# Sample state update of a gated recurrence by pairs of heads on four row groups of TensorE, in a one-core decoder layer

## The chip, the cores and the metric

The kernel runs on one core of a Trainium2 chip. Its time is device microseconds of one execution; the figure used is the median of several runs. Each execution of the program is one launch.

## What is computed

The reference is one layer of a hybrid decoder for a prompt group (1 x 1024 tokens) and a sample group (8 sequences x 8 tokens) that share weights: a first SwiGLU block, a mixer, a second SwiGLU block. The mixer projects with `w_in`, runs sliding-window attention on one part and a gated linear recurrence with four heads on another, and projects back with `w_out`. Everything is f32. The part that matters here is the recurrence (`hgrn2_chunked`) of the sample group, whose state (8 sequences x 4 heads x 128 x 128) comes in as `state_hgrn` and goes out updated:

```
A = jnp.einsum('bhtk,bhsk,bhtsk->bhts', qb, kb, decay)
o = jnp.einsum('bhts,bhsv->bhtv', A, vb) + jnp.einsum('bhtk,bhkv->bhtv', qb * jnp.exp(G), S)
S = jnp.exp(G_last[:, :, 0, :])[..., None] * S + jnp.einsum('bhsk,bhsv->bhkv', kb * jnp.exp(G_last - G), vb)
```

For a sample sequence there is one chunk of 8 tokens: the new state of a head is its old state, scaled row by row, plus keys (8 x 128) transposed times values (8 x 128).

## The kernel before, in words

**Tiling.** Tokens are cut into three blocks: block 0 holds 256 prompt tokens and the 64 sample tokens (width 320), blocks 1 and 2 hold 384 prompt tokens each. Projections are done as three products of split f32 halves (`mm3`, L276 to L280): one full-array matmul each on L278, L279 and L280. These carry most of the time of TensorE.

**Order.** The source is written as one stream of projection and FFN units with generators beside it. `stream` and `tick` (L96 to L107) let a generator (the mixer of a block, normalisations) advance by one step at fixed rates while units go by. A scheduler of the framework then orders the instructions of each engine by its own model of time and gives tiles their slots; an instruction whose slot is not free is put later. So what stands together in the source need not stand together on the engine. Each engine then runs its list in order and waits on semaphores. SP issues nearly all transfers, in order.

**Banks.** PSUM has eight banks of 128 x 512 f32: four with the tag `mm` (`mmbank`, L60) for the projections, four with the tag `ax` (`axbank`, L63) for everything that the generators do. Around the change the projections in turn are those of block 1: `w_in_units(1)` (L1049). Its `tr` (L1054) is a unit of 24 matmuls of 384 columns into one `mm` bank, taken out by VectorE on L1060; the value projection (L1098 to L1108) uses three `mm` banks at once for 72 matmuls of 512 columns. Weights come by SP in 512 KB loads into three raw slots and are split by ScalarE (L257) and VectorE (L258).

**The sample update.** `sample_hgrn` (L1401) runs as part of the mixer of block 0, beside `sample_attn` (L1322), whose output goes through DRAM (`osc`, L1390 and L1395) before `finish_attn` (L1121) ends it, and beside the normalisation of block 1 (`pre_n`, L443, its transposes on L467). `intra` (L1207) makes the chunk's inner products `At`, the scaled queries `Q`, keys `K` and the decay `D`, all with channels on the 128 partitions. Then:
- L1409 transposes the keys of the four heads, each 128 x 64 to 64 x 128, into one bank; L1411 copies them to `kn` (64 partitions, tokens).
- For each head `a`: L1415 loads its state (512 KB); L1417 (GpSimd) masks the queries by sequence; L1420 (VectorE) builds `vb`, the head's values repeated four times and masked so that each copy keeps one sequence of each half (`seqm`, L200); L1425 and L1429 add the output products into `sav`, on halves of 32 tokens; L1431 (GpSimd) scales the state by `D`; L1435 multiplies keys and masked values of each half (32 rows, 512 columns: four sequences at once) into an `ax` bank, `su`; L1437 (VectorE) adds that to the state; L1438 stores it.

So the eight `su` products of L1435 use rows 0 to 31 and 32 to 63 of the array, the partitions on which the 64 sample tokens lie. The values come from the projection of block 0: `z["v"]`, third row tile, partitions 0 to 63 (L1106 to L1108).

Of the kernel before, what the change touches and what calls it, by code (L numbers as in the profile page):

```python
# [8 lines left out]
F32 = mybir.dt.float32  # L9
# [9 lines left out]
P = 128  # L19
# [25 lines left out]
def tile_step(ctx: ExitStack, tc: tile.TileContext, A: dict, O: list):  # L45
# [82 lines left out]
    amask = cp.tile([P, 256], F32, name="amask")  # L128
    smask = cp.tile([P, 136], F32, name="smask")
    ssink = cp.tile([P, 2], F32, name="ssink")  # L130
    seqm = cp.tile([NS, 4], F32, name="seqm")
    lmask = {h: cp.tile([P, 32], U8, name=f"lm{h}") for h in LEVELS[2:]}
    ident32 = cp.tile([P, 32], F32, name="ident32")
    lb = cp.tile([P, 4], F32, name="lb")
# [32 lines left out]
    def mix_consts():  # L167
# [852 lines left out]
    def mixing(tp, h):  # L1020
# [28 lines left out]
        def w_in_units(n):  # L1049
            w = WIDTH[n]  # L1050
            npb = NPB[n]
            z = Z[n] = {}

            def tr(c, dst):  # L1054
                wt = col_tile(c)
                bank = mmbank()
                proj(bank[:, :w], wt, h[n], w, range(4))
                tick()
                proj(bank[:, :w], wt, h[n], w, range(4, 8))
                V.tensor_scalar(dst, bank[:, :w], bias(c), None, op0=ALU.add)  # L1060
# [36 lines left out]
            S.activation(z["hq"][:, :, :w], z["hq"][:, :, :w], AF.Silu)  # L1097
            hv = z["v"] = big(F32, (P, 3, 512))  # L1098
            banks = [mmbank() for _ in range(nb)]
            for kk in range(4):  # L1100
                ap = w_in[kk * 256:(kk + 1) * 256, 1792:2304].rearrange("(k p) m -> p k m", p=P)
                wt = load_w([(None, ap)], pp, "wsp", 8, (P, 2, 512))
                proj_tok(banks, wt, h[n], n, (2 * kk, 2 * kk + 1))
                tick()
                tick()
            for i in range(nb):  # L1106
                r = rows_of(n, i)
                V.tensor_tensor(hv[:r, i], banks[i][:r], bhi[:r], op=ALU.add)  # L1108
# [98 lines left out]
        def intra(n, c0, r, top, last_q, res):  # L1207
# [193 lines left out]
        def sample_hgrn():  # L1401
# [2 lines left out]
            res = []  # L1404
            yield from intra(n, c0, r, 4, True, res)
            At, Q, K, D = res
            tb = axbank("skT").rearrange("p (a t) -> p a t", a=4)
            for a in range(4):
                PE.transpose(tb[:r, a], K[:, a, :r], ident)  # L1409
            kn = t2((P, 4, P))  # L1410
            V.tensor_copy(kn[:r], tb[:r])  # L1411
            ob = axbank("sav")
            for a in range(4):
                st = big(F32, (P, 8, P))
                nc.sync.dma_start(st, A["state_hgrn"][0][:, a].rearrange("b k v -> k b v"))  # L1415
                qm = t2((P, 2, 4, 32))
                G.tensor_tensor(qm, Q[:, a, :r].rearrange("p (f t) -> p f t", f=2).unsqueeze(2).to_broadcast(  # L1417
                    [P, 2, 4, 32]), own.unsqueeze(1).to_broadcast([P, 2, 4, 32]), op=ALU.mult)
                vb = t2((P, 4, P))
                V.tensor_tensor(vb[:r], z["v"][:r, 2, a * P:(a + 1) * P].unsqueeze(1).to_broadcast([r, 4, P]),  # L1420
                                seqm.unsqueeze(2).to_broadcast([r, 4, P]), op=ALU.mult)
                yield
                sr = [slice(32 * hf, 32 * hf + 32) for hf in range(2)]
                for hf in range(2):
                    PE.matmul(ob[sr[hf], a * P:(a + 1) * P], At[:r, a, sr[hf]], z["v"][:r, 2, a * P:(a + 1) * P],  # L1425
                              start=True, stop=False, skip_group_check=True)
                for b in range(4):
                    for hf in range(2):
                        PE.matmul(ob[sr[hf], a * P:(a + 1) * P], qm[:, hf, b], st[:, 4 * hf + b], start=False,  # L1429
                                  stop=b == 3, skip_group_check=True)  # L1430
                G.tensor_tensor(st, st, D[:, a].unsqueeze(2).to_broadcast([P, 8, P]), op=ALU.mult)  # L1431
                yield
                for hf in range(2):
                    ub = axbank("su").rearrange("p (b t) -> p b t", b=4)
                    PE.matmul(ub, kn[sr[hf], a], vb[sr[hf]], start=True, stop=True)  # L1435
# [283 lines left out]
```

## Time and profile before

| what | value |
|---|---|
| median of three runs | 2006.6 us (2004.51 to 2008.71) |
| the profiled execution | 2007.94 us |
| its span in the profile | 2006.2 us |
| granted TensorE clock over the span | 0.999 |
| mean DMA rate | 185 GB/s |

The profile is of one execution, and its span leaves out what lies around the program's own instructions. The page gives busy time of each engine, the chain of waits that ended last, and groups of instructions by source line; further views of the trace list instructions in order of time, tabulate windows, or follow the chain through a stretch. PE is TensorE's matmuls, PEld its weight loads, DVE VectorE, ACT ScalarE, POOL GpSimd, SP the engine that issues transfers. An f32 matmul with f32 operands shows as two records. Ends of matmuls are modelled and they overlap, so prices on TensorE are read from start to start.

### The profile page before, as it was taken

How to read it: one execution, taken by the hardware profiler on the slowest of the kernel's cores; microseconds unless marked ns; L12 is line 12 of the kernel's file. 1: busy time of each engine (PE TensorE's matmuls, PEld its weight loads, DVE VectorE, ACT ScalarE, POOL GpSimd, SP SyncE). 2: the span in 40 equal slices, each digit the busy share in tenths (PEclk: the TensorE clock that was granted, in tenths of full speed). 3: DMA queues.
4: the chain of work that ended last, by engine and by line, in shares of the span. 5: the costliest groups of instructions: out<-in, count | busy, mean ns of one | idle time of the engine just before them, and what ended most of it. 6: DMA issues, size and time to landing. Idle time of an engine off the chain costs nothing.

```text
span 2006.2 us, 34709 instructions
## 1 busy us (share of the span) xinstructions
PE 1983.4 (99%) x13349; PEld 1856.0 (93%) x13349; DVE 1410.5 (70%) x2303; ACT 934.5 (47%) x1689; POOL 541.5 (27%) x508
## 2 busy tenths in 40 slices
PE   9999999999999999999999999999999999999998
PEld 8999999999998987798899898988999999999886
DVE  6676667887558655777667756857888878655666
ACT  7544333444455434435344544746544444444452
POOL 0013443655104101211212311220155565510201
PEclk9999999999999999999999999999999999999999
DMA  8545446566766756766434243527566555577874
GB/s 259 169 122 179 132 129 215 202 221 226 235 217 219 190 150 215 256 166 190 135 93 144 85 143 106 175 89 235 153 198 211 184 192 192 208 231 234 285 260 138
DMA packets 377319, 370.31 MB, mean 185 GB/s; under 512 B 40546, under 2 KB 294321, under 8 KB 377137
## 3 DMA queue, kind: packets, MB, share of 16 engines
q1 hardware_dynamic: 371169, 357.21, 56.2%
q10 hardware_dynamic: 5984, 10.88, 1.6%
q8 instruction: 105, 1.72, 0.4%
q14 instruction: 61, 0.50, 0.1%
HBM read 284.31 MB, written 84.71 MB: 184 GB/s over the span
## 4 chain that ended last, share of the span: by engine, by line
PE 87%; DVE 5%; DMA 5%; ACT 2%; issue 2%; SPq 0%; DVEq 0%; ACTq 0%
PE mm L278 26%; PE mm L280 25%; PE mm L279 25%; DMA raw<-in_ffn_w_gu_dram 2%; DMA ar<-act 2%; PE pv L1196 1%; PE c L278 1%; PE c L280 1%; PE c L279 1%; PE sc L1155 1%; DVE t L707 1%; DVE w L258 1%; PE pT L1183 1%; DVE wspl L258 1%; DMA ar<-fa 1%
## 5 line engine op out<-in xcount | busy, mean ns | idle before, releaser
L278 PE MATMUL mm<-h,wsph 128*128 128x320 f32 (+1 forms) x1296 | 412.1, 320 | 2.9 <-ACT wsph L257 1.3
L280 PE MATMUL mm<-h,wspl 128*128 128x320 f32 (+1 forms) x1296 | 409.1, 317 | 1.9 <-DVE wspl L258 1.8
L279 PE MATMUL mm<-h,wsph 128*128 128x320 f32 (+1 forms) x1296 | 409.6, 317 | 0.4 <-DVE h L258 0.4
L257 ACT CAST wsph<-raw 128x1024 fp32r<-128x1024 f32 x202 | 211.4, 1049 | 280.5 <-PE mm L279 211.9
L258 DVE TENSOR_TENSOR wspl<-raw,wsph 128x1024 fp32r<-128x1024 f32 x202 | 253.1, 1257 | 123.3 <-ACT wsph L257 120.7
L258 DVE TENSOR_TENSOR w<-raw,w 128x512 fp32r<-128x512 f32 (+1 forms) x214 | 223.9, 1050 | 87.4 <-ACT w L257 86.0
L257 ACT CAST w<-raw 128x512 fp32r<-128x512 f32 (+1 forms) x214 | 158.1, 742 | 216.1 <-PE mm L279 111.7
L278 PEld LDWEIGHTS mm<-h,wsph 128*128 128x128 f32 x1296 | 242.8, 188 | 7.4 <-issue 2.5
L280 PEld LDWEIGHTS mm<-h,wspl 128*128 128x128 f32 x1296 | 243.0, 188 | 5.8 <-DVE wspl L258 2.7
L279 PEld LDWEIGHTS mm<-h,wsph 128*128 128x128 f32 x1296 | 243.3, 188 | 2.4 <-issue 1.1
L278 PE MATMUL mm<-h,w 128*128 128x384 f32 x704 | 235.4, 335 | 1.5 <-DVE big L761 1.5
L279 PE MATMUL mm<-h,w 128*128 128x384 f32 x704 | 235.6, 335 | 0.0
L280 PE MATMUL mm<-h,w 128*128 128x384 f32 x704 | 230.2, 335 | 0.0
L278 PE MATMUL mm<-w,h 128*128 128x512 f32 x462 | 181.0, 395 | 1.1 <-DVE big L956 1.1
L745 POOL TENSOR_TENSOR big<-big 128x384 f32<-128x384 f32 x88 | 113.4, 1288 | 252.5 <-ACT big L758 143.8
L279 PE MATMUL mm<-w,h 128*128 128x512 f32 x462 | 181.1, 392 | 0.0
L280 PE MATMUL mm<-w,h 128*128 128x512 f32 x462 | 179.7, 391 | 0.0
L278 PE MATMUL mm<-big,w 128*128 128x384 f32 x528 | 176.8, 335 | 1.9 <-ACT big L748 1.1
L279 PE MATMUL mm<-big,w 128*128 128x384 f32 x528 | 176.5, 334 | 0.0
L280 PE MATMUL mm<-big,w 128*128 128x384 f32 x528 | 176.4, 334 | 0.0
L258 DVE TENSOR_TENSOR w<-t,w 128x512 fp32r<-128x512 f32 x176 | 160.7, 922 | 10.7 <-ACT w L257 10.3
L278 PEld LDWEIGHTS mm<-h,w 128*128 128x128 f32 x704 | 132.1, 188 | 1.8 <-DVE big L761 1.8
(358 smaller groups left out, 3854.6 us busy)
## 6 DMA issues: line engine op xcount, KB each, us to landing
raw<-in_ffn_w_gu_dram SPq DMA_DIRECT2D x156, 512.0 KB
raw<-in_ffn_w_down_dram SPq DMA_DIRECT2D x74, 512.0 KB
raw<-in_w_in_dram SPq DMA_DIRECT2D x54, 512.0 KB
ar<-fa SPq DMA_DIRECT2D x70, 384.0 KB
big<-in_ffn_w_down_dram SPq DMA_DIRECT2D x88, 256.0 KB
fb<-big SPq DMA_DIRECT2D x44, 512.0 KB
fa<-big SPq DMA_DIRECT2D x22, 768.0 KB
raw<-fb SPq DMA_DIRECT2D x30, 512.0 KB
```

What stands on the lines that cost most here:

```text
L257: S.copy(hi, src)
L258: (lo_eng or V).tensor_tensor(lo, src, hi.bitcast(F32), op=ALU.subtract)
L278: PE.matmul(out, a[0], b[0], start=first, stop=False, skip_group_check=resume)
L279: PE.matmul(out, a[0], b[1], start=False, stop=False, skip_group_check=resume)
L280: PE.matmul(out, a[1], b[0], start=False, stop=last, skip_group_check=resume)
L707: V.tensor_tensor(t, x, y, op=ALU.subtract)
L745: G.tensor_tensor(e[:, i], e[:, i], e[:, i + 1], op=ALU.mult)
L1155: PE.matmul(banks[g][:, i * 256:i * 256 + wk], zq[64 * g:64 * g + 64, 2 * pr + i, b * P:(b + 1) * P], kx[64 * g:64 * g + 64, k0:k0 + wk], ...
L1183: PE.transpose(bank[:, (i * nk + kb) * P:(i * nk + kb + 1) * P], pt[g][:, i, kb * P:(kb + 1) * P], ident)
L1196: PE.matmul(ob[:, hd * 64:hd * 64 + 64], pT[g][:, (i * nk + kb) * P:(i * nk + kb + 1) * P], vn[:, vb, g * 64:g * 64 + 64], start=kb == 0, ...
```

## The change

The four heads are taken in two pairs. The even head's keys and values stay on partitions 0 to 63; the odd head's go to partitions 64 to 127.
- After the value projection of block 0, one transfer on SP copies the values of heads 1 and 3 (64 x 2 x 128, 64 KB) from partitions 0 to 63 to the unused partitions 64 to 127 of the same tile, at the place of heads 0 and 2.
- `seqm` is built for 128 partitions instead of 64.
- `K` is made 64 wide for the sample block, so that the keys of two heads lie next to each other. Two transposes of 128 x 128 take the place of four of 128 x 64, and the copy to `kn` is 128 x 256 instead of 64 x 512.
- `vb` is built once for a pair, on 128 partitions, ahead of both heads' steps: two builds instead of four.
- Within a pair, both heads' output products and state scalings come first. The four `su` products follow, on rows 0, 32, 64 and 96 of the array, into two `ax` banks and two `mm` banks. Then come the four additions, with a store of each head's state after its second one. The even head's products go to the `ax` banks, the odd head's to the `mm` banks.

```diff
-    seqm = cp.tile([NS, 4], F32, name="seqm")
+    seqm = cp.tile([P, 4], F32, name="seqm")
...
-        V.tensor_scalar(seqm, tf[:NS, 3, 0:4], tf[:NS, 2, 64:65], None, op0=ALU.is_equal)
+        V.tensor_scalar(seqm, tf[:, 3, 0:4], tf[:, 2, 64:65], None, op0=ALU.is_equal)
...
                 V.tensor_tensor(hv[:r, i], banks[i][:r], bhi[:r], op=ALU.add)
+            if n == 0:
+
+                odd, even = [hv[sl, 2].rearrange("p (q o c) -> p q o c", o=2, c=P) for sl in (slice(0, NS), slice(NS, P))]
+                nc.sync.dma_start(even[:, :, 0], odd[:, :, 1])
...
-            Q, K, D = t2((P, 4, P)), t2((P, 4, P)), t2()
+            Q, K, D = t2((P, 4, P)), t2((P, 4, r)), t2()
...
-            for a in range(4):
-                PE.transpose(tb[:r, a], K[:, a, :r], ident)
-            kn = t2((P, 4, P))
-            V.tensor_copy(kn[:r], tb[:r])
+            for p in range(2):
+                PE.transpose(tb[:, p], K[:, 2 * p:2 * p + 2].rearrange("p a t -> p (a t)"), ident)
+            kn = t2((P, 2, P))
+            V.tensor_copy(kn, tb[:, :2])
...
-                vb = t2((P, 4, P))
-                V.tensor_tensor(vb[:r], z["v"][:r, 2, a * P:(a + 1) * P].unsqueeze(1).to_broadcast([r, 4, P]),
-                                seqm.unsqueeze(2).to_broadcast([r, 4, P]), op=ALU.mult)
...
+            for p in range(2):
+                vb, sts = t2((P, 4, P)), []
+                V.tensor_tensor(vb, z["v"][:, 2, 2 * p * P:2 * p * P + P].unsqueeze(1).to_broadcast([P, 4, P]),
+                                seqm.unsqueeze(2).to_broadcast([P, 4, P]), op=ALU.mult)
+                for a in (2 * p, 2 * p + 1):
...
-                for hf in range(2):
-                    ub = axbank("su").rearrange("p (b t) -> p b t", b=4)
-                    PE.matmul(ub, kn[sr[hf], a], vb[sr[hf]], start=True, stop=True)
-                    sl = st[:, 4 * hf:4 * hf + 4]
-                    V.tensor_tensor(sl, sl, ub, op=ALU.add)
-                nc.sync.dma_start(O[7][0][:, a].rearrange("b k v -> k b v"), st)
+                ubs = [axbank("su"), axbank("su"), mmbank(), mmbank()]
+                for i, ub in enumerate(ubs):
+                    rows = slice(32 * i, 32 * i + 32)
+                    PE.matmul(ub, kn[rows, p], vb[rows], start=True, stop=True)
+                for i, ub in enumerate(ubs):
+                    sl = sts[i // 2][:, 4 * (i % 2):4 * (i % 2) + 4]
+                    V.tensor_tensor(sl, sl, ub.rearrange("p (b t) -> p b t", b=4), op=ALU.add)
+                    if i % 2:
+                        nc.sync.dma_start(O[7][0][:, 2 * p + i // 2].rearrange("b k v -> k b v"), sts[i // 2])
```

The output products, the query masks and the scalings of the state keep their form inside the head's steps.

More of the change, by code (lines that the diff above doesn't have):

```diff
@@ L1407, in sample_hgrn @@
             tb = axbank("skT").rearrange("p (a t) -> p a t", a=4)
-            for a in range(4):
-                PE.transpose(tb[:r, a], K[:, a, :r], ident)
-            kn = t2((P, 4, P))
-            V.tensor_copy(kn[:r], tb[:r])
+            for p in range(2):
+                PE.transpose(tb[:, p], K[:, 2 * p:2 * p + 2].rearrange("p a t -> p (a t)"), ident)
+            kn = t2((P, 2, P))
+            V.tensor_copy(kn, tb[:, :2])
             ob = axbank("sav")
[L1413 to L1418, printed above, removed]
-                vb = t2((P, 4, P))
-                V.tensor_tensor(vb[:r], z["v"][:r, 2, a * P:(a + 1) * P].unsqueeze(1).to_broadcast([r, 4, P]),
-                                seqm.unsqueeze(2).to_broadcast([r, 4, P]), op=ALU.mult)
-                yield
-                sr = [slice(32 * hf, 32 * hf + 32) for hf in range(2)]
-                for hf in range(2):
-                    PE.matmul(ob[sr[hf], a * P:(a + 1) * P], At[:r, a, sr[hf]], z["v"][:r, 2, a * P:(a + 1) * P],
-                              start=True, stop=False, skip_group_check=True)
-                for b in range(4):
-                    for hf in range(2):
[L1429 to L1433, printed above, removed]
-                    ub = axbank("su").rearrange("p (b t) -> p b t", b=4)
-                    PE.matmul(ub, kn[sr[hf], a], vb[sr[hf]], start=True, stop=True)
-                    sl = st[:, 4 * hf:4 * hf + 4]
-                    V.tensor_tensor(sl, sl, ub, op=ALU.add)
-                nc.sync.dma_start(O[7][0][:, a].rearrange("b k v -> k b v"), st)
@@ new lines, in sample_hgrn @@
+            sr = [slice(32 * hf, 32 * hf + 32) for hf in range(2)]
+            for p in range(2):
[3 more added lines that the diff above has]
+                for a in (2 * p, 2 * p + 1):
+                    st = big(F32, (P, 8, P))
+                    sts.append(st)
+                    nc.sync.dma_start(st, A["state_hgrn"][0][:, a].rearrange("b k v -> k b v"))
+                    qm = t2((P, 2, 4, 32))
+                    G.tensor_tensor(qm, Q[:, a, :r].rearrange("p (f t) -> p f t", f=2).unsqueeze(2).to_broadcast(
+                        [P, 2, 4, 32]), own.unsqueeze(1).to_broadcast([P, 2, 4, 32]), op=ALU.mult)
+                    yield
+                    for hf in range(2):
+                        PE.matmul(ob[sr[hf], a * P:(a + 1) * P], At[:r, a, sr[hf]], z["v"][:r, 2, a * P:(a + 1) * P],
+                                  start=True, stop=False, skip_group_check=True)
+                    for b in range(4):
+                        for hf in range(2):
+                            PE.matmul(ob[sr[hf], a * P:(a + 1) * P], qm[:, hf, b], st[:, 4 * hf + b], start=False,
+                                      stop=b == 3, skip_group_check=True)
+                    G.tensor_tensor(st, st, D[:, a].unsqueeze(2).to_broadcast([P, 8, P]), op=ALU.mult)
+                    yield
+                ubs = [axbank("su"), axbank("su"), mmbank(), mmbank()]
[7 more added lines that the diff above has]
+                        nc.sync.dma_start(O[7][0][:, 2 * p + i // 2].rearrange("b k v -> k b v"), sts[i // 2])
```

## The prediction

> **What bounds the kernel now.** I read the page first: the busy shares and the chain that ended last.
>
> ```profile
> span 2006.2 us, 34709 instructions
> PE 1983.4 (99%) x13349; PEld 1856.0 (93%) x13349; DVE 1410.5 (70%) x2303; ACT 934.5 (47%) x1689; POOL 541.5 (27%) x508
> PE 87%; DVE 5%; DMA 5%; ACT 2%; issue 2%; SPq 0%; DVEq 0%; ACTq 0%
> ```
>
> TensorE is busy for all but 23 us, and 87% of the chain is its own work. That is an average, so I asked for the stretch that the change touches: from the keys' transposes (L1409, at 902.40) to the last instruction that the update feeds (L1282, over by 981.45), as a table of windows.
>
> ```profile
> 902.40:981.45 79.05, 79.05 (x500) 65.80 (x498) 57.12 (x115) 37.20 (x64) 14.39 (x17) 1.00 0.60 176
> 912.70:933.00 20.30, 20.30 (x162) 16.57 (x160) 19.23 (x45) 12.52 (x19) 3.94 (x3) 1.00 0.76 220
> ```
>
> The columns are length, then busy time of PE, PEld, DVE, ACT and POOL, granted clock, DMA share, GB/s. TensorE has no idle moment in 79 us and runs at full clock. VectorE is close behind between 912.7 and 933 (19.23 of 20.30 us), but TensorE does not wait for it. So a step here is worth what it adds to or takes from TensorE's queue, as long as no new wait appears. Then I asked for the chain of waits over 890 to 1000; it stays on TensorE in this stretch, and names each piece of the sample update:
>
> ```profile
> 913.96 1.00 PE sav L1429 x16
> ...
> 920.53 1.06 PE su L1435 x4
> ...
> 929.57 0.78 PE sav L1429 x12
> ...
> 931.38 0.34 PE sav L1429 x4
> ...
> 939.73 1.05 PE su L1435 x2
> ...
> 941.22 0.55 PE sav L1429 x6
> 941.77 1.05 PE su L1435 x2
> 942.82 0.34 PE sav L1429 x4
> ...
> 943.64 0.56 PE sav L1429 x6
> ...
> 955.01 1.06 PE su L1435 x4
> ...
> 964.24 1.06 PE su L1435 x4
> 965.30 1.00 PE sav L1429 x16
> ```
>
> Each f32 matmul is two records. The eight products `su` stand in five places: three places hold two (x4), two places hold one (x2). **A place costs 1.05 us whether it holds one product or two**: two products on different row groups already run side by side.
>
> **What the change does to the order.** The source puts four `su` products behind each other, on four row groups. The built program does not keep them together, and I looked at its instruction order for that. In the first pair of heads, the two products of the odd head (those in the main banks) stand together, 126 rows of TensorE's order ahead of the two of the even head, which stand alone, with four full matmuls between. In the second pair all four stand alone, with 31, 14 and 18 full matmuls between them. That makes seven places instead of five. Before this stretch the order of TensorE is the same row for row, and behind it too. The prices of the rest come from the timeline of TensorE:
>
> ```profile
> 902.40 0.60 PE L1409 MATMUL skT<-ident,t 128*64 128x128 f32 x4
> 902.75 0.42 PE L278 MATMUL mm<-h,wsph 128*128 128x384 f32 x1
> ...
> 913.25 0.27 PE L1374 MATMUL spT<-ident,t 128*128 128x128 f32 x1
> 913.35 0.27 PE L1375 MATMUL spT<-ident,t 128*8 128x128 f32 x1
> 913.55 0.41 PE L1425 MATMUL sav<-big,At 64*32 64x128 f32 x4
> 913.89 1.07 PE L1429 MATMUL sav<-big,t 128*32 128x128 f32 x16
> 914.89 0.41 PE L1425 MATMUL sav<-big,At 64*32 64x128 f32 x4
> 915.23 0.44 PE L278 MATMUL mm<-h,wsph 128*128 128x384 f32 x1
> 915.51 0.34 PE L279 MATMUL mm<-h,wsph 128*128 128x384 f32 x1
> ...
> 925.23 0.87 PE L467 MATMUL tr<-ident,big 128*128 128x128 f32 x6
> 925.86 0.42 PE L280 MATMUL mm<-h,wspl 128*128 128x384 f32 x1
> ...
> 938.89 0.39 PE L279 MATMUL mm<-wspl,h 128*128 128x512 f32 x1
> 939.12 0.39 PE L280 MATMUL mm<-wsph,h 128*128 128x512 f32 x1
> 939.34 0.39 PE L278 MATMUL mm<-wsph,h 128*128 128x512 f32 x1
> 939.66 1.12 PE L1435 MATMUL su<-t,t 32*128 32x512 f32 x2
> ```
>
> Matmuls are pipelined, so the price is from start to start. Sixty full 384-column matmuls take 902.75 to 913.25, 0.175 us each; a 512-column one takes 0.23.
> - **`su` products:** two places more, 2 x 1.05 = **+2.10**.
> - **Keys' transposes:** four of 64 columns take 0.35 (902.40 to 902.75). Two of 128 columns take 2 x 0.105, from the six in 0.63 at 925.23: **-0.14**.
> - **`sav` products (L1429):** a head's 16 records cost 1.00 in one piece; the second head's cost 0.78 + 0.34 and the third's 0.55 + 0.34 + 0.56, since other work cuts them. All four sum to 4.57. In the new order three are whole and one is cut once by a transpose: 3 x 1.00 + 1.2 = 4.2, **-0.37**.
> - **Crossings:** the first full matmul behind a small tile takes 0.28 (915.23 to 915.51) instead of 0.175, and the last one ahead of a small tile 0.32 (939.34 to 939.66) instead of 0.23: 0.2 for each piece of small work between full matmuls. I count 14 such pieces in the old order, 16 in the new: **+0.40**.
>
> [...]
>
> Sum: 2.10 - 0.14 - 0.37 + 0.40 = **+2.0 us**. The profiled execution took 2007.94 us (its span is 2006.2, 1.7 lie around it), so it would be 2009.9. The median of the three runs is 2006.6, 1.3 below that execution, so I forecast **2008.6 us**.
>
> **What I cost at nothing, and its cover.** VectorE loses two builds of the masked values and half of the key copy:
>
> ```profile
> 909.42 0.68 DVE L1411 COPY t<-skT 64x512 f32<-64x512 f32 x1
> ...
> 914.60 0.68 DVE L1420 TENSOR_TENSOR t<-big,seqm 64x512 f32<-64x512 f32 x1
> ...
> 919.94 0.60 DVE L1060 TENSOR_SCALAR big<-mm,cols 128x384 f32<-128x384 f32 x1
> ...
> 935.37 0.28 DVE L1389 TENSOR_SCALAR t<-spv,sm 128x64 f32<-128x64 f32 x1 [2.52 <-PE spv L1386]
> ...
> 948.08 0.15 DVE L1125 TENSOR_SCALAR sm<-sm 64x1 f32<-64x1 f32 x1
> ```
>
> That is about 2 us of VectorE, and TensorE waits for none of it: nothing gained. Three new waits of TensorE matter, since everything of the input projection is queued behind them on TensorE.
> 1. The first two `su` products now wait for the masked values. VectorE has the key copy at 909.42 (0.35 to 0.68, now 256 columns), an L1060 (0.60) and the build (0.68 to 1.05): done by 911.1 to 911.8. TensorE gets there at 902.4 + 0.21 + 57 x 0.175 = 912.6. Slack about 1 us.
> 2. These products sit in two of the four main banks until VectorE's additions, some 20 us later, so the projection's units turn over the two that are left. The third unit from there waits for the eviction (L1060) of the first. TensorE is there after su 1.05, 36 full matmuls (6.3), spT 0.30, two L1425 (0.68), L1429 (1.00) and three crossings (0.6): 922.5. The eviction stands at the same place of VectorE's queue as the L1060 at 919.94: done at about 920.6. Slack 2 us.
> 3. The second product of the second pair waits for the addition out of its bank, which on VectorE stands behind L1125, the end of the sample attention. From L1389 to L1125 it is 12.7 us now (935.37 to 948.08), mostly the round trip of the attention's output. The new order reaches that L1389 at about 944, so L1125 comes at 956.7 and the addition is done by 958; TensorE, counted as above, is there at 960. Slack 2 us.
>
> Where VectorE is later than these slacks, each microsecond costs TensorE one; I take 0, with the range up to the second rival's price.
>
> The copy of the odd heads' values is one transfer of 64 KB more, on SP, behind the last L1108 of the first block:
>
> ```profile
> 716.30 19.17 SPq L931 DMA_DIRECT2D raw<-fb  x6
> ...
> 722.40 0.68 DVE L1108 TENSOR_TENSOR big<-mm,bhi 64x512 f32<-64x512 f32 x1 [0.69 <-PE mm L280]
> ```
>
> SP issues six loads in 19.17 us here, so it mostly waits; the load behind the copy waits for an L258 that follows this L1108 on VectorE anyway. At most it costs an issue and 64 KB at the page's mean rate, under 1 us; I take 0. The wider mask and the narrower key tile issue nothing more. The state loads of the second pair move up and the state stores change places on SP; each still goes out before its product or after its addition is due, at no cost as long as the waits above have slack.
>
> **Rivals.**
> - *The update does what it says* (4%): the products of a pair run as one place of 1.05. Two places for five give -3.15, with the two small gains -3.7: 2002.9 us. Against it: the built order keeps them apart.
> - *The main banks run short* (14%), the case on the slower side. VectorE is at 95% from 912.7 to 933. If it is 4 us late there or behind the attention's round trip, two of the three slacks are used up and TensorE stands for 2 us twice: 2.0 + 4.0 = +6.0, 2012.6 us. It decides when an eviction is more than 2 us later than worked out. For it: the third wait hangs on small transfers. Against it: VectorE has less to do than before. [...]
> - *The 2 us vanish later* (12%): some wait of TensorE behind 981 is set by a transfer that does not move, and takes up to 1.5 us of it: 2007.1 us. Against it: 87% of the chain is TensorE, and a load waits for buffers that TensorE frees.
> - *The forecast* (70%): 2008.6 us.
>
> **How the numbers follow.** A measurement of this kernel tells about 0.2% (4 us) from no change; the three runs lie 4.2 us apart. The forecast is +0.1%, within that bound; a run-to-run shift of 2 us either way stays mostly inside. Faster by over 0.2%: the first rival and 3% from the spread, 0.07. Slower: the second rival and 7% from the forecast's upper tail, 0.21. Within 0.2%: 0.72. The range goes from the forecast less 4 to the second rival, 2004.6 to 2012.6; it leaves out the first rival and a little beyond each end.
>
> **What would show it.** The profile after should have `su` in seven places of 1.05 us each, `sav` in four pieces of about 1.00 with one cut, full matmuls unchanged at 0.175 and 0.23, no idle of TensorE in the stretch, and its end (the last L1282) about 2 us later against the same start. I am wrong if `su` runs in fewer or cheaper places, if TensorE is idle there for an addition or an eviction, or if the end moves by something that this stretch does not show.

## The result, and the profile after

| | before | after |
|---|---|---|
| median, us | 2008.28 (2004.51 to 2011.91, 14 runs) | 2011.05 (2008.65 to 2016.51, 14 runs) |
| the profiled execution, us | 2007.94 | 2012.91 |
| its span, us | 2006.2 | 2011.2 |
| granted TensorE clock over the span | 0.999 | 0.999 |

The ratio after to before is **1.0018, interval 1.0011 to 1.0025**: about 3.6 us slower (2.2 to 5.0), where +2.0 was forecast. (The two medians alone differ by 2.8 us; the text goes by the ratio and its interval.) The page after:

```profile
span 2011.2 us, 34706 instructions
...
PE 1987.8 (99%) x13347; PEld 1857.7 (92%) x13347; DVE 1410.4 (70%) x2301; ACT 934.2 (46%) x1689; POOL 546.7 (27%) x508
...
PE 88%; DVE 4%; DMA 4%; ACT 2%; issue 1%; SPq 1%; POOL 0%; ACTq 0%; DVEq 0%; POOLq 0%
```

The page tells almost nothing: TensorE has 4.4 us more of busy time, and the chain stays on it. The table of windows says more: first the stretch from the keys' transposes to the first output of the block behind, then the same 20.3 us as in the prediction. Columns: window, length, busy time of PE, PEld, DVE, ACT, POOL, clock, DMA share, GB/s.

```profile
903.33:986.25 82.92, 81.33 (x498) 66.24 (x496) 55.16 (x113) 37.09 (x64) 16.90 (x17) 1.00 0.57 168
912.70:933.00 20.30, 18.71 (x150) 15.17 (x148) 15.28 (x33) 12.02 (x19) 5.62 (x3) 1.00 0.64 194
```

The stretch took 79.05 us and now takes 82.92: **+3.87**. That is most of the 5.0 us by which the two spans differ; 0.93 lies ahead of the stretch, which is taken up below. In the first window PE is 1.59 us short of the length, in the second as well: TensorE stands there, where it did not stand before. Behind the stretch, to TensorE's last row, it is 1016.4 us before and 1016.6 after: nothing is given back later.

The timeline of TensorE shows both parts, the places of the products (the second mark in a row is the tile; a product in a main bank is named `mm`) and the two stalls:

```profile
913.55 1.13 PE L1443 MATMUL mm<-t,t 32*128 32x512 f32 x4
...
923.11 0.34 PE L280 MATMUL mm<-h,wspl 128*128 128x384 f32 x1
924.16 0.44 PE L278 MATMUL mm<-h,wsph 128*128 128x384 f32 x1 [0.71 <-DVE big L1060]
...
925.66 0.34 PE L280 MATMUL mm<-h,wspl 128*128 128x384 f32 x1
926.88 0.32 PE L1386 MATMUL spv<-kv,t 128*32 128x64 f32 x8 [0.88 <-DVE t L1381]
...
941.45 1.12 PE L1443 MATMUL su<-t,t 32*128 32x512 f32 x2
942.50 0.50 PE L279 MATMUL mm<-wspl,h 128*128 128x512 f32 x1
...
943.63 1.12 PE L1443 MATMUL su<-t,t 32*128 32x512 f32 x2
...
954.54 1.12 PE L1443 MATMUL mm<-t,t 32*128 32x512 f32 x2
...
962.85 1.12 PE L1443 MATMUL mm<-t,t 32*128 32x512 f32 x2
...
967.15 1.12 PE L1443 MATMUL su<-t,t 32*128 32x512 f32 x2
...
971.53 1.12 PE L1443 MATMUL su<-t,t 32*128 32x512 f32 x2
```

Seven places, 1.05 us each from start to start (941.45 to 942.50), as forecast. I added up the time from the start of each TensorE row to the start of the next over the whole stretch, by tile, with idle time apart:

| us | before | after | difference |
|---|---|---|---|
| products `su` (16 records) | 5.27 | 7.36 | +2.09 |
| idle | 0 | 1.59 | +1.59 |
| full matmuls (321), crossings included | 62.01 | 62.57 | +0.56 |
| sums `sav` | 5.92 | 5.68 | -0.24 |
| keys' transposes | 0.36 | 0.14 | -0.22 |
| all the rest | 5.50 | 5.60 | +0.10 |

So +2.3 us are the order of the work, nearly as forecast, and **+1.6 us are two stalls** that the forecast had at nothing. The experiments ask where the stalls come from. GpSimd's timeline of the kernel before, then VectorE's (the mask is L1417, the scaling L1431):

```profile
910.02 0.68 POOL L1417 TENSOR_TENSOR t<-t,own 128x256 f32<-128x256 f32 x1 [10.13 <-DVE big L438]
915.05 1.98 POOL L1431 TENSOR_TENSOR big<-big,t 128x1024 f32<-128x1024 f32 x1 [4.34 <-PE sav L1429]
```

```profile
915.20 1.85 DVE L244 TENSOR_TENSOR sm<-sm 128x3 f32<-128x3 f32 x1
...
918.61 0.27 DVE L1377 COPY t<-spT 128x128 f32<-128x128 f32 x1
```

And the same two of the changed kernel (mask L1428, scaling L1438):

```profile
915.50 1.73 POOL L1428 TENSOR_TENSOR t<-t,own 128x256 f32<-128x256 f32 x1 [14.68 <-ACT wsph L257]
920.75 2.62 POOL L1438 TENSOR_TENSOR big<-big,t 128x1024 f32<-128x1024 f32 x1 [3.52 <-PE sav L1436]
```

```profile
910.91 0.75 DVE L438 SCALAR_TENSOR_TENSOR big<-big,sm,xt 128x512 f32<-128x512 f32 x1 [1.33 <-DMA xt<-in_x_prompt_dram]
...
917.68 0.16 DVE L244 TENSOR_TENSOR sm<-sm 128x3 f32<-128x3 f32 x1
...
921.52 1.86 DVE L244 TENSOR_TENSOR sm<-sm 128x3 f32<-128x3 f32 x1
...
923.50 0.61 DVE L1060 TENSOR_SCALAR big<-mm,cols 128x384 f32<-128x384 f32 x1
...
924.21 1.28 DVE L459 TENSOR_SCALAR big<-big,sm 128x512 f32<-128x512 f32 x3
925.40 1.22 DVE L258 TENSOR_TENSOR wspl<-raw,wsph 128x1024 fp32r<-128x1024 f32 x1
926.54 0.28 DVE L1381 COPY t<-spT 128x128 f32<-128x128 f32 x1
```

Three things stand here. L244 works on 128 x 3 elements and takes 0.16 us; beside GpSimd's scaling of a state (L1431, now L1438) it takes 1.85, and ends with it. That happens before (917.05 us, the scaling at 917.03) and after (923.38 and 923.37); in e4 below, with the scaling on ScalarE, L244 takes 0.15. The traces show the longer instruction and the common end, not what in the chip makes VectorE wait. What is new is the time: GpSimd's mask of the queries starts 12.2 us behind the keys' transposes (903.33 to 915.50) instead of 7.6, its scaling 17.4 instead of 12.65. It now falls right ahead of an eviction (L1060) and of the copy of the attention's transposed weights (L1381) for which TensorE waits. The third thing is the first row: VectorE waits 1.33 us for a transfer there (L438), against 0.35 in the kernel before. This wait differs from profile to profile, 0.35 to 2.43 us over the kernels of the table below, and it delays VectorE too.

The mask is late because of its buffer. Small tiles take their slots in turn from a pool of eight. The change builds the masked values of a pair ahead of the mask of its first head, so the mask gets the next slot. In the built program that is the one of the attention's weights, and the mask has to wait for their transposes (L1378, L1379). Its row above names an L257 of ScalarE instead, which ended at 915.44, close to L1379 (915.27). In e4 below the mask starts 0.23 us behind L1379 as it does here, with the last L257 1.17 us back, so it is L1379 that releases it. Nothing in the source says so.

### The profile page after: what moved, and what is told of

Read it like the earlier page. It is cut to its first block, busy times and chain, and to the rows that moved or that the text cites. A ratio compares the mean times of both kernels' runs of the same rounds, so it can differ in the third digit from the quotient of the medians.

```text
span 2011.2 us, 34706 instructions
## 1 busy us (share of the span) xinstructions
PE 1987.8 (99%) x13347; PEld 1857.7 (92%) x13347; DVE 1410.4 (70%) x2301; ACT 934.2 (46%) x1689; POOL 546.7 (27%) x508
## 4 chain that ended last, share of the span: by engine, by line
PE 88%; DVE 4%; DMA 4%; ACT 2%; issue 1%; SPq 1%; POOL 0%; ACTq 0%; DVEq 0%; POOLq 0%
PE mm L278 26%; PE mm L280 26%; PE mm L279 26%; PE pv L1200 1%; PE c L278 1%; PE c L280 1%; PE c L279 1%; DMA ar<-act 1%; DMA ar<-fa 1%; PE sc L1159 1%; DVE w L258 1%; DMA big<-in_x_prompt_dram 1%; PE pT L1187 1%; PE lv L1232 1%; DVE t L707 0%
## 5 line engine op out<-in xcount | busy, mean ns | idle before, releaser
L257 ACT CAST wsph<-raw 128x1024 fp32r<-128x1024 f32 x202 | 211.3, 1049 | 279.1 <-PE mm L279 216.3
L258 DVE TENSOR_TENSOR wspl<-raw,wsph 128x1024 fp32r<-128x1024 f32 x202 | 250.9, 1246 | 124.1 <-ACT wsph L257 123.6
L258 DVE TENSOR_TENSOR w<-raw,w 128x512 fp32r<-128x512 f32 (+1 forms) x214 | 228.3, 1070 | 84.3 <-ACT w L257 82.7
L257 ACT CAST w<-raw 128x512 fp32r<-128x512 f32 (+1 forms) x214 | 158.0, 742 | 216.7 <-PE mm L279 112.5
L258 DVE TENSOR_TENSOR w<-t,w 128x512 fp32r<-128x512 f32 x176 | 162.6, 932 | 11.2 <-ACT w L257 11.0
```

Of the source, the lines that this page charges most:

```text
L257: S.copy(hi, src)
L258: (lo_eng or V).tensor_tensor(lo, src, hi.bitcast(F32), op=ALU.subtract)
```

## The experiments

My theory at first: two main banks are held, and VectorE is late behind the scaling, so the third unit finds no bank. The rival: VectorE is late for its own queue. The theory of the buffers came with the first results. Each time, the profiled execution gives the stretch (here between the same two rows) and the ratio comes from 5 to 11 runs (14 for the changed kernel) beside the kernel before on the same chip. "Rest" is the stretch less `su` and idle. The second kernel, e2, is not in the table, since its stretch ends at another place of the order.

| kernel | ratio, interval | stretch | `su` | idle | rest |
|---|---|---|---|---|---|
| before | | 79.05 | 5.27 | 0 | 73.8 |
| after | 1.0018, 1.0011 to 1.0025 | 82.92 | 7.36 | 1.59 | 74.0 |
| e1, copy alone | 1.0002, 0.9993 to 1.0011 | 79.59 | 5.27 | 0.24 | 74.1 |
| e3, no main banks | 1.0019, 1.0011 to 1.0028 | 84.44 | 7.36 | 1.65 | 75.4 |
| e7, scaling in quarters | 1.0011, 1.0002 to 1.0020 | 82.64 | 7.36 | 1.17 | 74.1 |
| e4, scaling on ScalarE | 1.0010, 1.0002 to 1.0019 | 80.76 | 7.36 | 0 | 73.4 |
| e15, mask first | 1.0025, 1.0016 to 1.0034 | 84.41 | 7.72 | 1.53 | 75.2 |
| e16, mask first, by head | 1.0015, 1.0006 to 1.0024 | 82.63 | 6.32 | 0.16 | 76.2 |
| e17, before, mask second | 1.0009, 1.0000 to 1.0018 | 82.44 | 5.27 | 2.15 | 75.0 |
| e18, before, scaling on ScalarE | 1.0003, 0.9994 to 1.0012 | 79.79 | 6.32 | 0 | 73.5 |
| e20, e17 and scaling on ScalarE | 1.0001, 0.9992 to 1.0009 | 79.18 | 5.27 | 0 | 73.9 |

The stretch starts at 900.6 to 903.3 us in all these profiles, and what lies behind it takes 1015.0 to 1017.4; so one profiled execution scatters by more than 1 us outside the stretch, and the 0.9 us by which the changed kernel is late at its start is within that.

**e1: the copy alone, in the kernel before.**

```diff
                 V.tensor_tensor(hv[:r, i], banks[i][:r], bhi[:r], op=ALU.add)
+            if n == 0:
+                odd, even = [hv[sl, 2].rearrange("p (q o c) -> p q o c", o=2, c=P) for sl in (slice(0, NS), slice(NS, P))]
+                nc.sync.dma_start(even[:, :, 0], odd[:, :, 1])
```

> The kernel before with nothing but the copy of the odd heads' values (64 KB on SP) added; its result is used by nothing. Theory (the copy is hidden): the keys' transposes start at 902.4 give or take 0.5 as in the kernel before, the stretch from them to the first output of the block behind stays 79.05 give or take 0.2 us, the ratio to the kernel before is 1.0000 give or take 0.0005. Rival (the copy delays the loads behind it and is the 0.9 us by which the changed kernel is late when the stretch begins): start at 903.3, stretch unchanged, time +0.9 us (ratio 1.0005).

Measured: start at 902.61, ratio 1.0002 (0.9993 to 1.0011). The stretch is 0.5 longer, not within 0.2: one wait of 0.22 ahead of L1385 and more cuts in the transposes. No cost of the copy shows; a rival of 0.9 us lies inside the interval of the ratio, but its sign, a late start, isn't there.

**e2: the two main-bank products ordered behind the other two.**

```diff
-                ubs = [axbank("su"), axbank("su"), mmbank(), mmbank()]
+                ubs, last = [axbank("su"), axbank("su"), mmbank(), mmbank()], None
...
-                    PE.matmul(ub, kn[rows, p], vb[rows], start=True, stop=True)
+                    with tc.issue_after(last) if last is not None else ExitStack():
+                        last = PE.matmul(ub, kn[rows, p], vb[rows], start=True, stop=True).ins
```

> The changed kernel with the two products in the main banks ordered behind the two in the other banks: the first pair's four products stand side by side, the second pair's as three and one, three places instead of seven; the projection gets no main bank while the two wait. Theory 1 for the price (a place costs 1.05 us whatever stands in it): the four take 1.0 to 1.1 us from start to start, the three as well. Rival for the price (only two products run beside each other): 2.1 us for the four. Theory 2 for the banks (held main banks stop TensorE): TensorE idle for 8 to 18 us in sum ahead of the four products, time 2014 to 2026 us in spite of 4.2 us less of products. Rival for the banks (the projection finds enough banks): no idle over 1 us, 2004 to 2007 us.

Measured: 2017.15 us, ratio 1.0055 (1.0041 to 1.0069). The timeline of TensorE at the second pair, then the first stall, and two windows behind it (the last column but two is the clock):

```profile
961.31 0.70 PE L1444 MATMUL su<-t,t 32*128 32x512 f32 x2
961.32 0.69 PE L1444 MATMUL mm<-t,t 32*128 32x512 f32 x1
961.84 0.59 PE L1444 MATMUL su<-t,t 32*128 32x512 f32 x2
961.85 0.59 PE L1444 MATMUL mm<-t,t 32*128 32x512 f32 x1
962.37 0.50 PE L278 MATMUL mm<-wsph,h 128*128 128x512 f32 x1
```

```profile
922.17 0.44 PE L1386 MATMUL spv<-kv,t 128*32 128x64 f32 x8 [6.03 <-DVE t L1381]
```

```profile
922.00:929.00 7.00, 5.57 (x50) 3.07 (x50) 4.39 (x14) 3.53 (x5) 2.56 (x2) 0.50 0.55 156
929.00:934.60 5.60, 4.65 (x16) 2.35 (x16) 3.33 (x9) 2.51 (x7) 0.00 (x0) 0.50 0.00 0
```

**Three products on three row groups take 1.06 us (961.31 to 962.37), the same as one.** So, for three products at least, the change would do what it says if the order let it. The price is the other half: while the two banks wait for their products no full matmul runs, TensorE stands for 8.4 us in sum, its clock is granted at 0.50, and the four products of the first pair take 2.7 us. The theory of the banks held: the products take 2.5 us less than in the changed kernel (4.83 in sum for 7.36), and the time is 11 us above the kernel before. For three products the theory of the price held; the four at a clock of 0.50 took 2.71 us (931.90 to 934.61), by an estimate from these two numbers 1.36 at the full one, so for four it isn't settled.

**e3: no main banks for the products.**

```diff
-                ubs = [axbank("su"), axbank("su"), mmbank(), mmbank()]
+                ubs = [axbank("su") for _ in range(4)]
```

> The changed kernel with all four products of a pair in the small work's banks, none in the main ones: seven places again, no main bank held. Theory (order +2.0 us, and 1.6 to 1.8 us of stalls because two main banks are held while VectorE is late): the two stalls of TensorE in the input projection (0.71 and 0.88 us, ahead of L278 and behind it) are gone or under 0.2 us in sum, the stretch from the keys' transposes to the first output of the block behind takes 81.1 give or take 0.4 us (before 79.05, changed 82.92), time 1.7 us below the changed kernel, 1.9 above the kernel before (ratio 1.0009). Rival (VectorE's late evictions stop TensorE with or without the held banks): the stalls stay at 1.2 us or more, stretch 82.5 or more, ratio 1.0018.

Measured: ratio 1.0019 (1.0011 to 1.0028), stretch 84.44: my theory fell. The stall for a bank is gone, but TensorE stands 1.65 us for the copy instead, and then has a mean clock of 0.57 over 4 us:

```profile
923.43 0.32 PE L1386 MATMUL spv<-kv,t 128*32 128x64 f32 x8 [1.65 <-DVE t L1381]
```

```profile
924.00:928.00 4.00, 4.00 (x22) 3.56 (x23) 3.16 (x6) 2.56 (x4) 0.76 (x1) 0.57 0.84 244
```

Held banks are not needed for a stall: VectorE is late (here it had waited 2.33 us at L438, and an L1091 beside the scaling took 2.05), and whatever TensorE needs of it next shows it.

**e7: the scaling as four instructions.**

```diff
-                    G.tensor_tensor(st, st, D[:, a].unsqueeze(2).to_broadcast([P, 8, P]), op=ALU.mult)
+                    for b in range(0, 8, 2):
+                        G.tensor_tensor(st[:, b:b + 2], st[:, b:b + 2], D[:, a, b:b + 2].unsqueeze(2).to_broadcast(
+                            [P, 2, P]), op=ALU.mult)
```

> The changed kernel with GpSimd's scaling of a head's state (2.62 us as one instruction) as four instructions of a quarter each; the order on TensorE is the same. Theory (VectorE's small L244, 1.86 us for 128x3 elements, stands behind GpSimd's scaling, and the eviction behind it comes too late for the two main banks that are left): the L244 beside the scaling takes 0.7 us or less, the eviction comes 1.2 us earlier, the two stalls (0.71 and 0.88 us) fall below 0.5 us in sum, the stretch falls from 82.92 to 81.7 or less, time 1.2 us below the changed kernel (ratio to the kernel before 1.0012). Rival (VectorE is late for its own queue, by the 1.33 us that it waits for a transfer at L438): L244 stays at 1.5 us or more or the stalls stay at 1.2 us or more, ratio 1.0018.

Measured: L244 0.57 us, but the L250 behind it 0.54 instead of 0.16, so VectorE still loses 0.8. The stall for the bank is gone; the one for the copy is 0.83 and 0.33 of short waits come later: 1.17 in sum, not under 0.5. Neither theory's number came; the ratio, 1.0011 (1.0002 to 1.0020), overlaps that of the changed kernel.

**e4: the scaling on ScalarE.**

```diff
-                    G.tensor_tensor(st, st, D[:, a].unsqueeze(2).to_broadcast([P, 8, P]), op=ALU.mult)
+                    for b in range(8):
+                        S.activation(st[:, b], st[:, b], AF.Copy, scale=D[:, a, b:b + 1])
```

> The changed kernel with the scaling of the states on ScalarE (eight instructions a head) instead of GpSimd; the order on TensorE and VectorE is that of the changed kernel until behind both stalls. Theory (VectorE loses 1.7 us behind GpSimd's scaling, and both stalls are that loss): L244 at 0.2 us or less, both stalls (0.71 and 0.88 us) under 0.3 us in sum, the stretch from the keys' transposes to the first output of the block behind 81.4 give or take 0.5 us (before 79.05, changed 82.92), ratio 1.0011. Rival (VectorE's own queue is late, whatever GpSimd does): 0.8 us of stall or more, stretch 82.2 or more, ratio 1.0015 or more.

Measured: the theory, with a stretch 0.14 us under its range. The timeline has the mask as late as ever, L244 short, and the eviction and the copy early; the window of the stretch has PE busy throughout:

```profile
912.75 0.70 POOL L1428 TENSOR_TENSOR t<-t,own 128x256 f32<-128x256 f32 x1 [14.68 <-PE spT L1379]
```

```profile
917.92 0.15 DVE L244 TENSOR_TENSOR sm<-sm 128x3 f32<-128x3 f32 x1
...
918.19 0.61 DVE L1060 TENSOR_SCALAR big<-mm,cols 128x384 f32<-128x384 f32 x1
...
921.24 0.28 DVE L1381 COPY t<-spT 128x128 f32<-128x128 f32 x1
```

```profile
900.58:981.34 80.76, 80.76 (x498) 66.06 (x496) 53.58 (x114) 45.97 (x96) 6.96 (x13) 1.00 0.58 172
```

TensorE doesn't stand for a moment. What is left against the kernel before, 1.7 us in the stretch and 1.0010 (1.0002 to 1.0019) in time, is the order with its seven places. The first row also names the mask's releaser: the transposes of the attention's weights (L1379).

Not all that VectorE gains here is the scaling's. The eviction starts 17.6 us behind the keys' transposes, in the changed kernel 20.2. Of these 2.6 us the L244 is 1.7; the other 0.85 stand already ahead of it, with a wait of 0.43 us at L438 in place of 1.33. By an estimate from the changed kernel's rows the 1.7 us alone would be enough: the eviction would be done at 922.4, with TensorE there at 923.45, and the copy at 925.1, with TensorE there at 925.3. For the copy that is enough by 0.2 only. The ratios of the two kernels overlap, so it is the profile, and not the time, that shows the stalls gone.

**e15: the mask ahead of the masked values, in the changed kernel.**

```diff
-                vb, sts = t2((P, 4, P)), []
-                V.tensor_tensor(vb, z["v"][:, 2, 2 * p * P:2 * p * P + P].unsqueeze(1).to_broadcast([P, 4, P]),
-                                seqm.unsqueeze(2).to_broadcast([P, 4, P]), op=ALU.mult)
+                sts = []
...
                         [P, 2, 4, 32]), own.unsqueeze(1).to_broadcast([P, 2, 4, 32]), op=ALU.mult)
+                    if a % 2 == 0:
+                        vb = t2((P, 4, P))
+                        V.tensor_tensor(vb, z["v"][:, 2, 2 * p * P:2 * p * P + P].unsqueeze(1).to_broadcast(
+                            [P, 4, P]), seqm.unsqueeze(2).to_broadcast([P, 4, P]), op=ALU.mult)
```

> The changed kernel with two statements exchanged: the mask of the queries (GpSimd, L1428) takes its buffer of the small tiles' pool ahead of the masked values instead of behind them. Seven places of products, two main banks held as in the changed kernel. Theory (the order of the buffers): in the changed kernel the mask gets the buffer of the attention's weights, waits for their transposes and starts 12.2 us behind the keys' transposes instead of 7.6; the sums of the first head, the scaling, and the copy of the transposed weights (L1381, whose buffer is the mask's) come late by it and stop TensorE. With the exchange the mask starts 7 to 8.5 us behind the keys' transposes, the copy is early, no stall over 0.2 us is left, stretch 81.3 give or take 0.4, ratio 1.0010. Rival (two held main banks stop TensorE): a stall of 0.7 us or more stays ahead of L278, stretch 82.0 or more, ratio 1.0014 or more.

Measured: the mask starts at 909.84, 7.6 us behind the transposes, and both stalls are gone. But the masked values now have the late buffer, and the products wait for them, behind an L258 that had waited 1.59 us for ScalarE, and again behind a scaling that falls on a tiny instruction of VectorE (L399, 1.86 us):

```profile
918.23 1.48 PE L1445 MATMUL mm<-t,t 32*128 32x512 f32 x4 [1.53 <-DVE t L1430]
```

```profile
915.31 1.86 DVE L399 SCALAR_TENSOR_TENSOR sm<-sm 128x3 f32<-128x3 f32 x1
```

Ratio 1.0025. The half of the theory that says where the two stalls come from held; that no stall would be left was wrong.

**e16: mask first, products by head.** As e15, and the products of a head behind its own scaling:

```diff
-                ubs = [axbank("su"), axbank("su"), mmbank(), mmbank()]
...
+                    for hf in range(2):
+                        ub = axbank("su").rearrange("p (b t) -> p b t", b=4)
+                        rows = slice(64 * (a % 2) + 32 * hf, 64 * (a % 2) + 32 * hf + 32)
+                        PE.matmul(ub, kn[rows, p], vb[rows], start=True, stop=True)
+                        sl = st[:, 4 * hf:4 * hf + 4]
+                        V.tensor_tensor(sl, sl, ub, op=ALU.add)
+                    nc.sync.dma_start(O[7][0][:, a].rearrange("b k v -> k b v"), st)
```

> The kernel of the exchanged statements with the products of each head issued behind its own scaling, as in the kernel before, all from the small work's banks; the odd heads' keys and values stay on the upper partitions. Six places of products (two, one, one, two, one, one). Theory (a place costs 1.05 us, and no stall without the late mask): su 6.3 us in sum, no stall over 0.3 us, stretch 79.9 give or take 0.5, ratio 1.0004. Rival (what costs is the row groups or the shared tiles, not the places): stretch 81 or more, ratio 1.0010 or more.

Measured: six places, 6.32 us, 0.16 of idle: both as the theory has it. But the stretch is 82.63 and the ratio 1.0015 (1.0006 to 1.0024), the rival's numbers. The windows show most of the reason:

```profile
961.00:964.00 3.00, 3.00 (x9) 1.25 (x9) 1.26 (x2) 0.32 (x2) 1.95 (x2) 1.00 0.06 14
964.00:968.00 4.00, 4.00 (x16) 3.98 (x14) 0.00 (x0) 0.00 (x0) 0.00 (x0) 0.57 0.46 133
```

TensorE had no idle at all there, and yet its clock falls in the second window, behind two places with one product each and a single full matmul between. By an estimate from the clock, those 4 us at 0.57 do 2.3 us of work: 1.7 us lost, of the 2.7 by which the stretch is over the theory. The other 1.0 was not followed up, so the rival isn't wholly excluded.

**e17: the kernel before, with the masked values ahead of the mask.** Two statements exchanged, nothing else:

```diff
-                qm = t2((P, 2, 4, 32))
-                G.tensor_tensor(qm, Q[:, a, :r].rearrange("p (f t) -> p f t", f=2).unsqueeze(2).to_broadcast(
-                    [P, 2, 4, 32]), own.unsqueeze(1).to_broadcast([P, 2, 4, 32]), op=ALU.mult)
                 vb = t2((P, 4, P))
...
+                qm = t2((P, 2, 4, 32))
+                G.tensor_tensor(qm, Q[:, a, :r].rearrange("p (f t) -> p f t", f=2).unsqueeze(2).to_broadcast(
+                    [P, 2, 4, 32]), own.unsqueeze(1).to_broadcast([P, 2, 4, 32]), op=ALU.mult)
```

> The kernel before with two statements exchanged and nothing else: the masked values take their buffer ahead of the mask of the queries, as in the changed kernel. Five places of products as before, no main bank held, none of the change in it. Theory (the order of the buffers makes the stall): the mask starts 11 us or more behind the keys' transposes instead of 7.6, TensorE stands 0.8 to 1.8 us ahead of L1382 for the copy of the transposed weights, with a low granted clock behind it if it stands for 1.6 us; stretch 80.0 to 82.0, ratio 1.0004 to 1.0015. Rival (the stalls belong to the grouping by pairs or to the held main banks): no stall over 0.3 us, stretch 78.3 to 79.2 (the sums of a head in fewer pieces), ratio 0.9996 to 1.0001.

Measured: the theory; the stretch, 82.44, is 0.4 over its range. On the timelines, and the window behind the stall:

```profile
913.44 0.68 POOL L1420 TENSOR_TENSOR t<-t,own 128x256 f32<-128x256 f32 x1 [14.96 <-ACT junk L393]
918.38 2.15 POOL L1431 TENSOR_TENSOR big<-big,t 128x1024 f32<-128x1024 f32 x1 [4.26 <-PE sav L1429]
```

```profile
918.30 2.45 DVE L1091 TENSOR_SCALAR big<-big,omlb,lb 128x384 f32<-128x384 f32 x2
...
923.60 0.29 DVE L1377 COPY t<-spT 128x128 f32<-128x128 f32 x1
```

```profile
923.95 0.32 PE L1382 MATMUL spv<-kv,t 128*32 128x64 f32 x8 [1.66 <-DVE t L1377]
```

```profile
926.00:930.00 4.00, 4.00 (x15) 3.79 (x13) 2.64 (x5) 0.88 (x2) 0.00 (x0) 0.57 0.27 89
```

The kernel before, with nothing of the change in it, stands 1.66 us for the copy; this time an L1091 pays beside the scaling (2.45 us for two that take 0.87 elsewhere). Another 0.49 ahead of L1374 was not followed up.

**e18 and e20: the scaling on ScalarE, in the kernel before and in e17** (the edit of e4).

> The kernel before with the scaling of the states on ScalarE instead of GpSimd; the mask keeps its early buffer; six places of products (one of the fourth head's stands alone). Theory (in the kernel before VectorE's loss beside GpSimd is covered, so taking it away gains nothing): L244 at 0.2 us or less, no idle of TensorE as before, stretch 79.9 give or take 0.5 us by the sixth place (before 79.05), ratio 1.0003. Rival (VectorE's loss also costs the kernel before): stretch 78.5 or less in spite of the sixth place, ratio 0.9995 or less.

> The kernel before with the two statements exchanged (masked values ahead of the mask of the queries, the late mask) and the scaling on ScalarE; five places of products. Theory (the late mask stops TensorE only because it puts GpSimd's scaling beside VectorE's urgent work): the mask is late, 11 us or more behind the keys' transposes, and yet the stall ahead of L1382 (1.66 us with the scaling on GpSimd) falls to 0.3 us or less, no low clock behind it, stretch 78.5 to 79.4, ratio 0.9999. Rival (the late mask stops TensorE by itself, through the copy that needs its buffer): a stall of 0.8 us or more, stretch 80 or more, ratio 1.0005 or more.

Measured: 79.79 us and 79.18 us of stretch, no idle in either, ratios 1.0003 (0.9994 to 1.0012) and 1.0001 (0.9992 to 1.0009). The mask of e20 is late, and nothing waits for it:

```profile
912.73 0.68 POOL L1420 TENSOR_TENSOR t<-t,own 128x256 f32<-128x256 f32 x1 [14.24 <-PE spT L1375]
```

With e17 this makes four corners: mask early or late, scaling on GpSimd or not. TensorE stands in one corner alone, late mask and scaling on GpSimd.

One thing was not held fixed over the corners. At L438 VectorE waited 2.43 us in e17 and 1.21 in e20. Behind the keys' transposes the copy comes 2.75 us earlier in e20 (19.87 for 22.62); 1.6 of this is the L1091 beside the scaling, 1.2 stands ahead of it. As an estimate from these rows, e17 without the 1.6 would stand 0.1 us for the copy, and without the 1.2 about 0.5. So the scaling is the larger part of the stall, and the wait for the transfer adds to it. In time e17 and e20 aren't told apart; their intervals overlap. No version beats the kernel before by what can be measured.

## Why the prediction was right, and where it failed

The sign and the range held, the size did not: 2008.6 us within 2004.6 to 2012.6 was forecast, 2011.05 was measured. The 2006.6 of three runs from which the forecast starts lies 1.7 below the 2008.28 of fourteen, and the loss itself is 3.6 us (2.2 to 5.0), not 2.0. That the time stayed in the range is in part luck: nothing in the sum stood for the stalls, and the ratio's interval reaches 1.0025, beyond the bound of 0.2%. By the prediction's own sign, "if TensorE is idle there for an addition or an eviction", its mechanism is wrong in one step, the slacks; the prices of the order were nearly right.

- **The places** were right: seven, at 1.05 each, +2.09 for +2.10. So was the ground for it: the built order keeps the four products apart, and three adjacent ones took 1.06 in e2, the price of one.
- **Transposes, `sav`, crossings**: -0.22, -0.24 and some +0.6 for -0.14, -0.37 and +0.40. The order as a whole is +2.3 by the changed kernel and +1.7 by e4, around the +2.0.
- **The copy at nothing**: no cost was found (e1), to within about 2 us of time.
- **Slack 1**, the masked values, held by a little. They were done at 913.2 and TensorE was there at 913.5:

```profile
912.51 0.68 DVE L1421 TENSOR_TENSOR t<-big,seqm 128x512 f32<-128x512 f32 x1
```

- **Slack 2, the third unit's bank, is the step that failed.** I took the eviction's time from the L1060 "at the same place of VectorE's queue", done at about 920.6. Its place was right, but its neighbours had moved: L244 with the scaling beside it now stands right ahead. The eviction was done at 924.1, 2.6 us later than worked out (the stretch starts 0.9 later), and TensorE waited 0.71. Of the 2.6 us, 1.7 are the L244; the rest stands ahead of it, where VectorE waits at L438 and for ScalarE (L1089). I had gone through TensorE's order for what moved, but not through GpSimd's, and I had not looked at which buffer each small tile gets. So neither the late mask nor the late scaling was in the forecast.
- **The copy of the attention's weights** was on no list of mine, so it was put at nothing without a reason: 0.88. Its buffer is the mask's, and on VectorE it is queued behind L459 and L258.
- **Slack 3** held; TensorE has no idle there.
- **The rival of the main banks** had the right sign and a right condition (an eviction over 2 us late), but the wrong root: without the banks the kernel stalls as much (e3), without the scaling it doesn't with them (e4).
- **The 2 us vanish later**: they don't, 1016.4 against 1016.6 us.

What stays open: why the clock falls in e16 and not in the changed kernel, how much of the runs' scatter is such falls, and how far the stalls change from run to run with VectorE's wait at L438.

## What to carry to other kernels

Before a wait is costed at nothing, list the order and the buffer of every tile in the pools that the edit allocates from, on all engines: one tile allocated earlier shifts the slots of the others, and a new wait arises between pieces of work that have nothing to do with each other. A slack of TensorE against VectorE was here only as good as what GpSimd did at that moment: an L244 of 0.16 us took 1.86 beside the scaling. And work that the source puts side by side must be looked for on the engine: here three products on three row groups took the time of one where they stood together (1.06 us in e2), and the changed kernel's order kept them apart.

## What the runs showed of the hardware

- **A place of small products had one price.** One, two or three f32 products of 32 x 512 on different row groups took 1.05 to 1.06 us at full clock (one in the changed kernel, 941.45 to 942.50; two in the kernel before, 954.94 to 956.00; three in e2, 961.31 to 962.37).
- **VectorE and GpSimd held each other up.** Beside a scaling of 2 to 2.6 us an L244 or L399 of 128 x 3 takes 1.85 to 1.86 us, and two L1091, which read one tile and two columns, take 1.6 more (2.44 us in e3 and 2.45 in e17 for 0.87). With the scaling on ScalarE the L244 takes 0.14 to 0.16 (e4, e18, e20). GpSimd loses as well: its mask takes 1.73 us in the changed kernel, where an L258 of VectorE started 0.03 us before it, and 0.68 in the kernel before. In e7 its four quarters let VectorE in between, at 0.57 and 0.54. What makes the one wait for the other, no run shows.
- **TensorE's clock fell to 0.50 without a long idle.** In e16 there was none ahead of it, only two places on 32 of the 128 rows; in e3, e15 and e17 1.5 to 1.7 us of idle with small work behind it. The changed kernel stood 0.71 and 0.88 and kept its clock, and so did e1 with an idle of 2.0 us between full matmuls near 492 us; so a stall of this length did not always bring a fall. In e3, e15, e16 and e17 the windows of one microsecond add up to the same loss, 1.7 us (3.4 us at half clock); in e3, e15 and e17 that is as much again as the stall ahead of it. In e2, with 8.4 us of idle in sum, the clock was 0.50 for 17 us (919 to 936). At 0.50 a full matmul of 384 columns takes 0.32 us from start to start (e3, 925.39 to 925.71), at full clock 0.17 (920.40 to 920.57). What sets a fall off, no run shows.
